# Interleaving the first two tiles of a retention and gMLP layer on eight cores

## The chip, the cores and the metric

The kernel runs on all 8 cores of one Trainium2 chip (trn2). Cores 0 to 3 are on one die, cores 4 to 7 on the other. Each core computes 4 of the 32 sequences and shares nothing with the others. The metric is the device time, in microseconds, of the slowest core.

Engines are named as in the profile: PE is the matmul engine, PEld its weight loads, DVE is VectorE, ACT is ScalarE, POOL is GpSimd, SP issues the DMA transfers. The trace also records the clock that PE was granted, as a share of full speed. A whole run can be in a slow state, with one die's clock clearly lower (in e1's run of 3871.15 us the cores of die 1 had a mean clock of 0.811 to 0.816, those of die 0 0.993 to 0.995); the runs are labelled with it. I call a core **undisturbed** when its mean granted clock over the execution is 0.991 or more, and an execution undisturbed when all eight cores are.

## The reference, cut to what matters

```python
D_MODEL, BATCH, SEQ, DEPTH = 1024, 32, 2048, 1
def reference(x, p, g_mix, w_in, ret_norm_g, sg_norm_g, w_s, b_s, w_out, ...):
    h = rmsnorm(x, g_mix[i])
    q, k, v, g, u, sv = jnp.split(h @ w_in[i], cuts, axis=-1)      # six columns of 512
    q = rotary(q.reshape(B, S, 4, 128), pos)
    k = rotary(k.reshape(B, S, 4, 128), pos) * 128 ** -0.5
    r = chunk_retention(q, k, v)                                   # recurrent over chunks
    r = layernorm_nogain(r).reshape(B, S, 512) * ret_norm_g[i]
    y_ret = jax.nn.silu(g) * r
    y_sg = spatial_gating(gelu(u), gelu(sv), w_s[i], b_s[i], sg_norm_g[i])
    x = x + jnp.concatenate([y_ret, y_sg], axis=-1) @ w_out[i]
    x = x + jnp.square(relu(rmsnorm(x, g_ffn[i]) @ w_ff1[i])) @ w_ff2[i]
    ...                                                            # gated embedding, final rmsnorm
```

## The kernel before

A core's 8192 tokens are 16 tiles of 512. Each tile goes through a *mixer* (the six projections of 512 columns, retention, gating), an output projection, a feed-forward and a gate. Weights come as *units* of 1024x512. On its first use a unit is read in float32 (2 MB, four *stage* pieces of 512 KB), multiplied by the norm's gain, converted to bf16 into a *ring* buffer, and written back to memory as bf16 (1 MB); later uses read those.

The program is scheduled on the host: every operation has a wanted time `vt`, the engines that may do it with a guessed duration, and the buffers it needs. A list scheduler simulates the engines and emits one fixed instruction order for each. Two things follow. Wanted times are priorities and not times on the chip. And any change of a duration or of an allowed engine reorders instructions everywhere.

The core of the scheduler. A DMA is a candidate as soon as its inputs and its buffer allow; nothing limits how far the queue runs ahead of the transfers:

```python
DMA_BW = 265e3
...
                    if op.ready > now + 1e-9:
                        continue
                    if e in op.lock and port[0] > now + 1e-9:
                        continue
                    if not can_alloc(op, now):
                        continue
```

The load of a unit: four pieces, the scaling on DVE or ACT (`both`), the write-back 20 us after in priority:

```python
        def load_unit(name, vt, cache=None):
            ...                                             # cut: ring buffer, cache of the first tiles
                for i in range(4):
                    s = g.buf("stage")
                    dma(lambda s=s: ap(s), lambda i=i: wf_d[u, :, i * 1024:(i + 1) * 1024], [], [(s, 0)], vt, ...)
                    if name in GAIN:
                        for j in range(2):
                            ...
                            g.add(both(512,
                                       lambda e, ...: e.tensor_scalar(
                                           out=o_(), in0=i_(), scalar1=gT[:, gc:gc + 1], scalar2=None, op0=ALU.mult),
                                       lambda e, ...: e.activation(
                                           out=o_(), in_=i_(), func=AF.Copy, scale=gT[:, gc:gc + 1])),
                                  [(s, 0), c("gT")], [(b, (i, j))], vt + 1, lock=("dve",))
                ...
                dma(lambda: wb_d[u], lambda: ap(b).rearrange("p k n -> p (k n)"), UB(b), [(wb_buf[name], 0)],
                    vt + 20, lambda: ("ws" + ring, b.slot), 1048576)
```

The projections of q and k, with the rotary: three products of a PSUM result on DVE and one sum on GpSimd for each of the eight heads:

```python
            for name, base in (("q", 0), ("k", 4)):
                u = load_unit(name, vt[0] - 25, cache)
                for h in range(4):
                    p = g.buf("psum")
                    g.add(mmgroup(lambda p=p: ps(p), lambda k, u=u, h=h: ap(u)[:, k, h * 128:(h + 1) * 128],
                                  lambda k: ap(n1T)[:, k, :], 8), UB(u) + A1, [(p, 0)], vt[0])
                    ...
                    g.add({"dve": (0.69, ... ap(m1) = ps(p) * cos            )}, ...)      # shortened
                    g.add({"dve": (0.69, ... ap(m2)[0:64] = ps(p)[64:] * sin )}, ...)
                    g.add({"dve": (0.69, ... ap(m2)[64:] = ps(p)[:64] * -sin )}, ...)
                    g.add({"pool": (1.27, ... ap(o) = ap(m1) + ap(m2)        )}, ...)
```

The normalisation of the retention result, on DVE, and the gain and gate products on GpSimd:

```python
                g.add({"dve": (1.6, nrm)}, [(bo, 0), (s2, "mv"), (s2, "r")], [(rn, 0)], vt[0])
                YR[b] = g.buf("y")
                g.add({"pool": (1.27, lambda e, o=YR[b]: e.tensor_tensor(out=ap(o), in0=ap(rn), in1=ap(GS[b]),
                                                                       op=ALU.mult))}, ...)
```

The order of the program: tile 0's mixer, tile 1's mixer, one output projection and one feed-forward for both, then a steady loop.

```python
        mixer(0, -195.0, 65.0, cache, True)
        mixer(1, -130.0, 65.0, cache, True)
        outproj([0, 1], -60.0, 50.0, True)
        ffn([0, 1], 0.0, 270.0)
        mixer(2, 30.0, 160.0)
        ...
```

## Time and profile before

| what | value | from |
|---|---|---|
| time, three runs | 3254.9, 3258.37, 3886.76 us | the runs; the last is slow |
| span of the undisturbed cores of the profiled execution (0 to 3) | 3236.9 us | cores, median |
| PE busy from 300 to 3100 us, core 1 | 2754.0 of 2800 us | busy time by stretch |
| first matmul, core 1 | 39.15 us | timeline of PE |
| start of the feed-forward, median of cores 0 to 3 | 196.2 us | trace: weight load number 805 |
| PE idle before that, median | 60.4 us | trace |

"Start of the feed-forward" is used through the whole document. All kernels here do the same 804 weight loads in the first two mixers and their output projection, so the start of the 805th marks the same point of the work in each.

The span and mean granted clock of each core, of the profiled execution before:

```profile
core 1: 3238.6 us, clock 0.994
...
die 0 (median of its cores): 3236.9 us, clock 0.994
die 1 (median of its cores): 3278.0 us, clock 0.980
```

Die 1 was disturbed, so core 1 is what I read. Its busy time by stretch; the columns are the stretch and its length, then busy us (and instructions) of PE, PEld, DVE, ACT and POOL, the granted PE clock, the busy share of the DMA engines, and GB/s:

```profile
0.00:40.00 40.00, 0.85 (x3) 0.32 (x4) 2.54 (x8) 18.19 (x26) 2.33 (x7) 1.00 0.91 268
40.00:160.00 120.00, 97.17 (x566) 49.30 (x565) 92.93 (x252) 59.67 (x89) 51.90 (x45) 0.93 0.86 262
160.00:199.00 39.00, 38.59 (x239) 19.82 (x238) 28.36 (x68) 24.69 (x38) 12.05 (x13) 1.00 0.47 163
300.00:3100.00 2800.00, 2754.01 (x14674) 1322.96 (x14673) 1638.19 (x3300) 988.10 (x1545) 593.37 (x550) 1.00 0.55 188
```

The last line is the steady state: PE is busy 98% of it, so it is bound by matmuls. The first three are the start: PE is idle for nearly all of the first 40 us, and for 22.8 of the next 120.

Why the first matmul is late is in the timeline of the DMA issues (start us, length of the issue, queue, line, operation, out<-in, count):

```profile
5.54 2.72 SPq L502 DMA_DIRECT2D xb<-x  x4
...
11.03 6.48 SPq L502 DMA_DIRECT2D xb<-x  x4
...
18.47 20.88 SPq L502 DMA_DIRECT2D stage<-wf  x8
39.40 0.54 SPq L502 DMA_DIRECT2D wb<-ring  x1
```

The first weights (wf) go out behind eight x blocks of 512 KB each, and the first write-back (wb) follows at once, while DMA is the scarce resource (busy share 0.91 in the first 40 us, 0.86 in the next 120). After the first matmul, PE waits for these, from 40 to 199 us on core 1 (who waits <- who is waited for: us in total, times, longest; the four largest):

```profile
PE ps L629 <- POOL qk L724: 7.4, 2, 7.0
PE ps L804 <- ACT Sbf L832: 5.7, 3, 2.2
PE ps L629 <- DVE y L945: 2.9, 2, 1.5
PE ps L804 <- DVE st L840: 2.7, 1, 2.7
```

L724 is the rotary sum on GpSimd, L832 a copy of the retention state, L945 the gating product, L840 a part of the normalisation.

### The profile page before, as it was taken

The numbers are of one execution on the slowest core, as the hardware profiler recorded it, in microseconds if no ns is written. First come the engines' busy times: TensorE is split into PE (matmuls) and PEld (weight loads), VectorE is DVE, ScalarE is ACT, GpSimd is POOL, SyncE is SP. The second block draws the span as 40 slices with busy tenths as digits, with TensorE's granted clock in tenths as the row PEclk, the third lists the DMA queues.
The fourth block names the chain that finished last, engine by engine and source line by source line (L and its number), as shares of the span: only waits on it lengthen the run. The fifth ranks groups of instructions, "written<-read, shape, count | busy, mean of one in ns | idle before, by whom it ended". The sixth has DMA issues, their size and how long they took to land.

```text
span 3281.8 us, 48876 instructions; the slowest of 8 cores (3231.4 to 3281.8 us)
## 1 busy us (share of the span) xinstructions
PE 3168.4 (97%) x16592; PEld 1511.0 (46%) x16592; DVE 1876.3 (57%) x3799; ACT 1185.6 (36%) x1837; POOL 681.9 (21%) x635
## 2 busy tenths in 40 slices
PE   4899998999999999999999999999999999999998
PEld 2444443444444444444444444444444444444444
DVE  3856656646556474564736656375564745647444
ACT  4563535233233332333324233342333323332233
POOL 1512102302213121131302213022130211313001
PEclk9899998999999999999999999999999999999999
DMA  9757755545546464464645546455464644645442
GB/s 275 240 194 249 255 191 195 210 152 199 186 172 214 147 220 167 166 224 155 219 154 180 199 161 221 160 183 202 169 208 149 217 164 177 218 154 187 149 170 86
DMA packets 113858, 618.31 MB, mean 188 GB/s; under 512 B 13136, under 2 KB 13392, under 8 KB 63440
## 3 DMA queue, kind: packets, MB, share of 16 engines
q1 hardware_dynamic: 113616, 615.19, 54.6%
q8 instruction: 139, 2.28, 0.3%
q14 instruction: 103, 0.84, 0.1%
HBM read 554.32 MB, written 60.82 MB: 187 GB/s over the span
## 4 chain that ended last, share of the span: by engine, by line
PE 94%; DMA 2%; ACT 1%; DVE 1%; issue 1%; SPq 1%; POOL 0%; DVEq 0%; ACTq 0%; POOLq 0%
PE ps L621 89%; PE ps L629 3%; DMA stage<-wf 2%; SPq L502 1%; ACT rel L1048 0%; PE ps L936 0%; PE ps L768 0%; PE ps L804 0%; PE ps L816 0%; PE ps L806 0%; ACT scr L927 0%; DVE TG L884 0%; ACT ring L577 0%; ACT ring L588 0%; DMA xb<-x 0%
## 5 line engine op out<-in xcount | busy, mean ns | idle before, releaser
L621 PE MATMUL ps<-TG,ring 128*128 128x512 bf16 x5120 | 1188.4, 386 | 56.2 <-ACT ring L577 39.3
L621 PE MATMUL ps<-ring,TG 128*128 128x512 bf16 x4096 | 984.0, 385 | 20.7 <-ACT rel L1048 10.7
L621 PE MATMUL ps<-ring,hT 128*128 128x512 bf16 x4096 | 926.7, 380 | 0.0
L621 PEld LDWEIGHTS ps<-TG,ring 128*128 128x128 bf16 x5120 | 501.0, 99 | 655.4 <-issue 140.1
L621 PEld LDWEIGHTS ps<-ring,TG 128*128 128x128 bf16 x4096 | 399.5, 99 | 498.6 <-issue 90.0
L1052 DVE TENSOR_TENSOR hT<-rel 128x512 bf16<-128x512 f32 x457 | 374.6, 820 | 420.8 <-ACT rel L1048 418.1
L621 PEld LDWEIGHTS ps<-ring,hT 128*128 128x128 bf16 x4096 | 395.4, 98 | 449.6 <-issue 11.7
L1048 ACT ACTIVATE rel<-ps 128x512 f32<-128x512 f32 x512 | 304.8, 596 | 755.3 <-PE ps L621 749.6
L1075 DVE SCALAR_TENSOR_TENSOR xb<-ps,st,xb 128x512 f32<-128x512 f32 x288 | 215.3, 747 | 275.6 <-PE ps L621 274.6
L724 POOL TENSOR_TENSOR qk<-scr 128x512 bf16<-128x512 f32 x128 | 163.8, 1280 | 873.7 <-DVE scr L721 873.7
L636 ACT ACTIVATE xsb<-xb 128x1024 bf16<-128x1024 f32 x200 | 210.5, 1052 | 330.2 <-DVE xb L1075 231.3
L1052 POOL TENSOR_TENSOR hT<-rel 128x512 bf16<-128x512 f32 x55 | 57.2, 1040 | 621.2 <-ACT rel L1048 621.1
L1119 ACT ACTIVATE gt<-ps,st 128x512 f32<-128x512 f32 x128 | 87.7, 686 | 220.2 <-PE ps L621 212.7
L993 DVE TENSOR_TENSOR xb<-xb,ps 128x512 f32<-128x512 f32 x128 | 87.8, 687 | 126.9 <-PE ps L621 120.0
L1125 DVE SCALAR_TENSOR_TENSOR gt<-gt,ps 128x512 f32<-128x512 f32 x128 | 87.8, 687 | 79.9 <-ACT gt L1119 78.7
L715 DVE TENSOR_TENSOR scr<-ps,rot 128x512 f32<-128x512 f32 x128 | 88.3, 690 | 67.9 <-PE ps L621 66.8
L871 POOL TENSOR_TENSOR y<-scr 128x512 bf16<-128x512 f32 x64 | 89.6, 1400 | 137.3 <-DVE scr L866 136.9
L1024 ACT ACTIVATE TG<-ps 128x1024 bf16<-128x1024 bf16 x75 | 76.7, 1024 | 108.9 <-PE ps L629 91.9
L945 DVE SCALAR_TENSOR_TENSOR y<-ps,bsT_s,scr 128x128 bf16<-128x128 f32 x256 | 72.0, 344 | 52.7 <-ACT scr L927 26.9
L788 POOL TENSOR_TENSOR scr<-scr,retgh 128x512 f32<-128x512 f32 x64 | 81.6, 1275 | 92.0 <-DVE scr L785 91.9
L905 ACT ACTIVATE scr<-ps,st 128x512 f32<-128x512 f32 x64 | 43.6, 687 | 157.5 <-PE ps L621 157.5
L866 DVE TENSOR_SCALAR scr<-ps,st 128x128 f32<-128x128 f32 x256 | 87.3, 405 | 18.7 <-POOL st L857 18.7
(79 smaller groups left out, 2379.0 us busy)
## 6 DMA issues: line engine op xcount, KB each, us to landing
ring<-wb SPq DMA_DIRECT2D x366, 1024.0 KB, 5.5
stage<-wf SPq DMA_DIRECT2D x104, 512.0 KB, 8.1
stage<-xT SPq DMA_DIRECT2D x64, 512.0 KB, 7.4
xb<-x SPq DMA_DIRECT2D x64, 512.0 KB, 5.5
out<-xb SPq DMA_DIRECT2D x64, 512.0 KB, 3.7
stage<-x SPq DMA_DIRECT2D x56, 512.0 KB, 10.8
wb<-ring SPq DMA_DIRECT2D x26, 1024.0 KB, 9.3
rot<-ROT SPq DMA_DIRECT2D x16, 512.0 KB, 6.1
```

The costliest lines, as they stand in the source:

```text
L621: r = e.matmul(out(), lhs(k), rhs(k), start=(start + k == 0), stop=(start + k == total - 1))
L629: r = e.transpose(out=psb(outb)[:, k * 128:(k + 1) * 128], in_=srcf(k), identity=ident[:, :])
L636: g.add({"act": (t_act(1024) + 0.19, lambda e: e.activation(out=ap(j), in_=ap(xbuf), func=AF.Square, accum_out=acc()))}, [(xbuf, 0), (xbuf ...
L715: g.add({"dve": (0.69, lambda e, p=p, m1=m1: e.tensor_tensor(out=ap(m1), in0=ps(p), in1=ap(rotb)[:, 0, :], op=ALU.mult))}, [(p, 0), (rotb, ...
L724: g.add({"pool": (1.27, lambda e, m1=m1, m2=m2, o=o: e.tensor_tensor(out=ap(o), in0=ap(m1), in1=ap(m2), op=ALU.add))}, [(m1, 0), (m2, 0), ...
L871: g.add({"pool": (1.27, lambda e, o=YR[b]: e.tensor_tensor(out=ap(o), in0=ap(rn), in1=ap(GS[b]), op=ALU.mult))}, [(rn, 0), (GS[b], 0)], [( ...
L993: g.add({"dve": (0.69, lambda e, p=p, xx=xx, hsl=hsl: e.tensor_tensor(out=ap(xx)[:, hsl], in0=ap(xx)[:, hsl], in1=ps(p), op=ALU.add))}, [( ...
L1048: g.add({"act": (t_act(512), lambda e, p=p, r=r: e.activation(out=ap(r), in_=ps(p), func=AF.Relu))}, [(p, 0)], [(r, 0)], vt[0])
L1052: fsq = lambda e, r=r, o=o: e.tensor_tensor(out=ap(o), in0=ap(r), in1=ap(r), op=ALU.mult)
L1075: e.scalar_tensor_tensor(out=ap(xx)[:, hsl], in0=ps(fbb), scalar=stc(s4, 8 + b), in1=ap(xx)[:, hsl], op0=ALU.mult, op1=ALU.add))},
L1119: g.add({"act": (t_act(512) + .1, lambda e, p=p, gt=gt, b=b: e.activation(out=ap(gt), in_=ps(p), func=AF.Tanh, scale=stc(st, 12 + b)))}, [ ...
L1125: g.add({"dve": (0.69, lambda e, p2=p2, gt=gt: e.scalar_tensor_tensor(out=ap(gt), in0=ap(gt), scalar=1.0, in1=ps(p2), op0=ALU.add, op1=ALU ...
```

## The change

The intent is to shorten the start. q's weights and tile 0's transposed x go out first, q's matmuls run by quarters as the pieces land, and the two mixers are interleaved so that each unit that arrives feeds two tiles. Write-backs are put off until the weights are in. The scheduler holds a DMA back while more than 4 us of transfers are queued, so that priorities decide what goes out. Tile 1's rotary and the retention's normalisation may leave DVE, and GpSimd may scale weights too. Line numbers of the kernel after are shifted against those of before: its matmuls are L627 (before L621), its transposes L635 (before L629). Not shown in the cut: a third rotary table, other buffers for tile 1's q, k and v, and a small DVE operation per block that prepares the bias for the normalisation on ACT.

```diff
+DMA_AHEAD = 4.0
@@ the scheduler
+                    if op.dma is not None and dma_free[0] > now + DMA_AHEAD:
+                        heapq.heappush(events, dma_free[0] - DMA_AHEAD)
+                        continue
@@ constants and identity: wanted 15 to 20 us later
-        cload("KD", KD[:, :], KD_d[:, :], VT0 - 10)
+        cload("KD", KD[:, :], KD_d[:, :], VT0 + 10)
@@ load_unit
-                    dma(... wf_d[u, :, i * 1024:(i + 1) * 1024], [], [(s, 0)], vt,
+                    dma(... wf_d[u, :, i * 1024:(i + 1) * 1024], [], [(s, 0)],
+                        vt + (2 * i if name == "q" else 0),
...
-                            g.add(both(512, <dve>, <act>),
-                                  [(s, 0), c("gT")], [(b, (i, j))], vt + 1, lock=("dve",))
+                            g.add(both(512, fts, <act>, fts),                       # fts: DVE or GpSimd
+                                  [(s, 0), c("gT")], [(b, (i, j))], vt + 1, lock=("dve", "pool"))
...
-                    vt + 20, lambda: ("ws" + ring, b.slot), 1048576)
+                    vt + (80 if cache is not None else 20), lambda: ("ws" + ring, b.slot), 1048576)
@@ mixer
+                pieces = t == 0 and name == "q"
+                if pieces:
+                    for i in range(4):
+                        for h in range(4):
+                            g.add(mmgroup(..., 2, start=2 * i, total=8),
+                                  [(u, (i, 0)), (u, (i, 1)), (n1T, i)], [(P4[h], 0)], vt[0] + i)
...
+                    if early and t:                                                 # tile 1's rotary
+                        for i in range(2):
+                            g.add({"act": (t_act(512), ... ap(m2)[lo, :] = ps(p)[hi, :])}, ...)
+                        g.add({"pool": (1.27, ... ap(m2) = ap(m2) * rot(1))}, ..., lock=("pool",))
+                    else:
                         <the two DVE products as before>
...
+                def nrma(e):
+                    for h in range(4):
+                        r = e.activation(out=ap(rn)[:, hs], in_=ps(bo)[:, hs], func=AF.Identity,
+                                         scale=stc(s2, 36 + h), bias=stc(s2, h))
-                g.add({"dve": (1.6, nrm)}, [(bo, 0), (s2, "mv"), (s2, "r")], [(rn, 0)], vt[0])
+                g.add({"dve": (1.6, nrm), "act": (1.2, nrma)}, [(bo, 0), (s2, "mv"), (s2, "r"), (s2, "s6")], [(rn, 0)],
+                      vt[0])
@@ the program
-        mixer(0, -195.0, 65.0, cache, True)
-        mixer(1, -130.0, 65.0, cache, True)
+        mixer(0, -195.0, 100.0, cache, True, xs_vt=-3.0, xt_vt=-30.0)
+        mixer(1, -185.0, 125.0, cache, True, "hT", "hT", xs_vt=-2.0, xt_vt=-28.0)
```

## The prediction

> **What bounds the kernel now.** On core 1, an undisturbed die, the span is 3238.6 us. Busy time by stretch shows TensorE (PE) busy 2754 of the 2800 us from 300 to 3100 us: matmul-bound, DMA at 55%. The start is not. From 0 to 199 us, where the first feed-forward matmul starts, PE is busy 136.6 us and idle 62.4:
> - 39.2 us before the first matmul. The waits put it on the scaling of the first weight unit; the timeline of DMA issues shows why: rotary table, eight x blocks and constants (about 6.5 MB) go out ahead of the q weights, which follow from 18.5 us, with DMA already at 97-100%.
> - about 23 us in pieces up to 160 us: 7.0 on the GpSimd add of the rotary, 5.7 on the state copy, 2.7 on normalisation, the rest on transposes and sums. VectorE is 96% busy in many 5 us slices; DMA is 91-97% busy from 20 to 100 us, at 266-298 GB/s.
>
> **What the change does.**
> 1. q weights and transposed x go first, each quarter of q used as it lands. Only about 2 MB must land before the first matmul. Estimate from 290 GB/s, 1.5 us of issue, 0.7 us of scaling: first matmul at 11-13 us, tile 0's q done at 22-25. That q runs at DMA rate, then tile 1's transposed x (2 MB, 7 us) is awaited: 20-26 us of PE idle by 40 us, against 39.
> 2. Interleaving gives each 2 MB unit (7.3 us of DMA) eight groups (13.9 us of PE), so PE, not DMA, should pace from about 35 us.
> 3. Deferred write-back moves 6 MB (about 21 us of DMA) behind the last unit; DMA is now nearly idle at 160-170 and 190-213 us. Moved, not saved; the feed-forward after it runs at 234-312 GB/s.
> 4. Tile 1's rotary: 16 VectorE products of 0.69 us become 16 ScalarE copies[...] and 8 GpSimd products of 1.28 us. The normalisation (1.6 us of VectorE per block) may go to ScalarE. VectorE, 124 us busy in the first 199, should fall to 100-113; GpSimd, 66, should rise to 76 or more. A q or k unit costs GpSimd 4x1.27 + 4x2.55 = 15.3 us, more than PE's 13.9: some waiting moves there.
>
> Steady state gains little; the 9 us stop near 500 us (x buffers awaiting output) is untouched.
>
> [...] granted clock 0.50 at 60-65 us, after a 7 us gap.
>
> **On the critical path.** Ideally, PE-paced after 35 us, the feed-forward starts near 158 us (41 saved). Dependencies through VectorE and GpSimd, and DMA shared with write-backs, should give back about 10. I expect it near 167 us: 32 us saved.
>
> **Predicted time: 3226 us, range 3206 to 3246.** All startup idle is 62 us, 1.9%, so over 2% is nearly out of reach. Faster by over 2%: 0.03; within 2%: 0.96; slower: 0.01.
>
> **What would show it.** Step 1: first matmul at 10-14 us. Step 2: PE idle in 40-160 us at 8-15 us instead of 23. Step 3: no write-backs before about 80 us. Step 4: VectorE below 113 us busy in the first 199 us, GpSimd above 75. Sum: the same later stages, about 32 us earlier.
>
> **What would make it wrong.** GpSimd or ScalarE becomes the pacer; the capped DMA lookahead starves the queue; deferred write-backs hold ring buffers, so later weights are late and the gain is given back by 400 us; or the changed instruction order moves steady-state stalls.

Two passages are cut, where marked: an estimate for ScalarE's copies (measured in after: 0.59 us each, L749, core 1) and a sentence on the clock; the granted clock of 0.50 beside it is from the trace of before. The forecast's sum: 199 - 158 = 41 us ideally, about 10 given back, 32 us saved, and 3258.37 - 32 = 3226 us. Figures close to those of the estimate in point 1 are in the trace of before, core 1: 289 GB/s from 40 to 60 us, the first transposed x issued at 1.51 us, 0.71 us for a scaling on ACT (L577). So are those of point 2: 2.1 MB at 289 GB/s are 7.3 us, and 64 matmuls at the pace of the 40 from 117.42 us (0.216 us each) are 13.8 us.

## The result, and the profile after

Four runs of the changed kernel took 3222.24 to 3224.33 us, median 3223.7, all fast and all undisturbed. The kernel before took 3254.9 and 3258.37 us in its two fast runs; its other two, 3620.93 and 3886.76, were slow. The ratio of after to before is 0.9898 (0.9874 to 0.9922). Ratios here are the mean time of one kernel's fast runs over that of the other's fast runs of the same rounds, so they are not quite the ratios of the medians that I quote.

**That ratio is not like for like.** On the chip of experiment e6, the fast runs of the kernel before took 3255.7 to 3264.0 us, and in each of them at least one pair of cores ran at clock 0.985 to 0.987 while the others had 0.993 to 0.996. In the run of 3260.45 us, cores 0 and 1 had spans of 3258.9 and 3258.1 us at 0.985 and cores 2 to 7 spans of 3233.5 to 3239.8 us. Where no pair was disturbed, the same kernel took 3240.7 to 3245.6 us (16 executions on several chips), median 3243.4. The four runs of the kernel after carry no disturbed core. The clocks of the first two runs of before were not kept, so that they had such a pair is inferred from their length. Undisturbed against undisturbed, the gain is 3243.4 - 3223.7 = 19.7 us, 0.6%, and not 33. A repeat on a chip where before ran undisturbed gave that directly: ratio 0.994 (after_again, below).

The two dies of the profiled execution after, and core 1 by the same stretches as before:

```profile
die 0 (median of its cores): 3219.7 us, clock 0.994
die 1 (median of its cores): 3221.1 us, clock 0.993
```

```profile
0.00:40.00 40.00, 17.64 (x63) 6.84 (x63) 13.43 (x19) 17.59 (x21) 7.90 (x11) 0.91 0.91 262
40.00:160.00 120.00, 102.87 (x625) 52.35 (x624) 86.73 (x257) 79.61 (x134) 89.12 (x74) 0.94 0.84 257
160.00:199.00 39.00, 39.00 (x230) 19.65 (x229) 21.40 (x38) 29.78 (x47) 7.47 (x5) 1.00 0.80 253
300.00:3100.00 2800.00, 2752.42 (x14633) 1320.68 (x14631) 1576.03 (x3138) 1043.13 (x1730) 573.60 (x539) 1.00 0.54 188
```

The steady state has not moved (2752.4 us of PE against 2754.0). The first 40 us gained 16.8 us of PE. From 40 to 160 us PE gained only 5.7, while GpSimd went from 51.9 to 89.1 us busy and ACT from 59.7 to 79.6.

The DMA issues of core 1 after:

```profile
1.50 1.36 SPq L507 DMA_DIRECT2D stage<-xT  x3
2.91 1.58 SPq L507 DMA_DIRECT2D stage<-wf  x1
4.54 0.67 SPq L507 DMA_DIRECT2D rot<-ROT  x1
10.79 0.33 SPq L507 DMA_DIRECT2D stage<-xT  x1
11.72 5.14 SPq L507 DMA_DIRECT2D stage<-wf  x3
...
51.70 0.33 SPq L507 DMA_DIRECT2D stage<-IDENT  x1
...
63.76 0.58 SPq L507 DMA_DIRECT2D wb<-ring  x1
```

The order is the one intended, and the first write-back is now issued at 63.8 us. But nothing is issued between 41.1 and 51.7 us: the queue waits 7.3 us for ACT and 3.2 us for GpSimd to convert pieces and so free stage buffers, and the transfers fall to 164 GB/s from 50 to 60 us. What PE did in that time on core 1 (start us, length, then the idle time before it and its releaser):

```profile
16.64 3.57 PE L627 MATMUL ps<-TG,ring 128*128 128x512 bf16 x8 [16.64 <-ACT ring L583]
20.66 5.84 PE L627 MATMUL ps<-TG,ring 128*128 128x512 bf16 x24 [0.44 <-ACT ring L583]
31.77 22.64 PE L627 MATMUL ps<-TG,ring 128*128 128x512 bf16 x96 [5.27 <-ACT TG L681]
```

q of tile 0 is done at 26.5 us; then PE waits 5.3 us for tile 1's transposed x, the input of the next matmuls. After that, its waits are spread over many lines (40 to 179 us, core 1; the four largest):

```profile
PE ps L635 <- POOL y L925: 4.9, 3, 2.5
PE ps L627 <- ACT scr L919: 2.9, 1, 2.9
PE ps L856 <- DVE Sst L867: 1.6, 1, 1.6
PE ps L627 <- DVE ring L580: 1.3, 1, 1.3
```

The wait of 7 us is gone. At the head are now GpSimd's product of gate and normalised retention (L925) and the normalisation that the change put on ACT (L919).

The account over all undisturbed cores, medians, in us (4 cores before, 8 after); medians of parts do not add up exactly to the median of the whole. "Lost to the clock" is the time before the feed-forward times the part of the clock that was not granted. It is an upper bound of the cost, since PE is idle for part of these stretches; the line under it counts only the time in which PE was busy.

| | before | after | difference |
|---|---|---|---|
| first matmul | 38.9 | 15.1 | -23.8 |
| PE idle, 0 to 40 us | 38.9 | 21.7 | -17.2 |
| PE idle, 40 to 130 us | 16.5 | 16.5 | 0.0 |
| PE idle, 130 us to the feed-forward | 4.6 | 0.2 | -4.4 |
| PE busy until the feed-forward | 136.6 | 140.4 | +3.8 |
| (lost to the clock) | 8.5 | 10.2 | +1.7 |
| (lost to the clock while PE was busy) | 5.3 | 8.4 | +3.1 |
| **start of the feed-forward** | **196.2** | **178.6** | **-17.6** |
| from there to the end | 3039.7 | 3042.0 | +2.3 |
| DVE / ACT / POOL busy until the feed-forward | 123.6 / 102.5 / 66.2 | 111.2 / 110.2 / 102.5 | |

So some 17 of the 22 us of idle time saved come from the first 40 us, none from the 90 us in which the interleaving was to work, 4.4 us from the last stretch, and 3.8 us are given back in busy time, most of it (3.1 us) at a lowered clock.

### The profile page after: what moved, and what is told of

It is laid out like the page before. It is cut to its first block, busy times and chain, and to the rows that moved or that the text cites. A ratio compares the mean times of both kernels' runs of the same rounds, so it can differ in the third digit from the quotient of the medians.

```text
span 3222.5 us, 49142 instructions; the slowest of 8 cores (3216.9 to 3222.5 us)
## 1 busy us (share of the span) xinstructions
PE 3125.9 (97%) x16592; PEld 1498.3 (46%) x16592; DVE 1813.2 (56%) x3636; ACT 1244.8 (39%) x2045; POOL 716.0 (22%) x662
## 4 chain that ended last, share of the span: by engine, by line
PE 93%; DMA 2%; ACT 1%; POOL 1%; issue 1%; DVE 1%; SPq 0%; DVEq 0%; ACTq 0%; POOLq 0%
PE ps L627 89%; PE ps L635 3%; DMA stage<-wf 1%; DMA stage<-xT 1%; ACT rel L1102 0%; DMA xb<-x 0%; PE ps L990 0%; PE ps L808 0%; PE ps L844 0%; POOL ring L580 0%; PE ps L846 0%; PE ps L856 0%; ACT scr L981 0%; ACT scr L919 0%; POOL y L925 0%
## 5 line engine op out<-in xcount | busy, mean ns | idle before, releaser
L627 PE MATMUL ps<-TG,ring 128*128 128x512 bf16 x5120 | 1164.5, 380 | 38.9 <-ACT ring L583 16.8
L627 PE MATMUL ps<-ring,TG 128*128 128x512 bf16 x4096 | 974.2, 382 | 24.4 <-ACT rel L1102 10.7
L627 PE MATMUL ps<-ring,hT 128*128 128x512 bf16 x4096 | 923.2, 379 | 0.0
L627 PEld LDWEIGHTS ps<-TG,ring 128*128 128x128 bf16 x5120 | 495.6, 98 | 622.6 <-issue 48.8
L627 PEld LDWEIGHTS ps<-ring,TG 128*128 128x128 bf16 x4096 | 396.9, 98 | 494.4 <-issue 44.9
L627 PEld LDWEIGHTS ps<-ring,hT 128*128 128x128 bf16 x4096 | 393.7, 98 | 442.9
L764 POOL TENSOR_TENSOR qk<-scr 128x512 bf16<-128x512 f32 x120 | 154.5, 1287 | 855.3 <-DVE scr L761 792.1
L1047 DVE TENSOR_TENSOR xb<-xb,ps 128x512 f32<-128x512 f32 x128 | 87.9, 687 | 127.5 <-PE ps L627 120.8
L755 DVE TENSOR_TENSOR scr<-ps,rot 64x512 f32<-64x512 f32 x120 | 83.2, 693 | 63.6 <-PE ps L627 62.6
L925 POOL TENSOR_TENSOR y<-scr 128x512 bf16<-128x512 f32 x64 | 81.5, 1274 | 161.3 <-ACT scr L919 156.1
L919 ACT ACTIVATE scr<-ps,st 128x128 f32<-128x128 f32 x224 | 84.3, 459 | 69.0 <-DVE st L902 69.0
L828 POOL TENSOR_TENSOR scr<-scr,retgh 128x512 f32<-128x512 f32 x64 | 81.2, 1269 | 92.3 <-DVE scr L825 89.7
L975 POOL TENSOR_TENSOR svn<-scr,sgg_s 128x512 bf16<-128x512 f32 x64 | 81.7, 1276 | 69.5 <-DVE scr L971 59.8
```

What stands on the lines that cost most here:

```text
L627: r = e.matmul(out(), lhs(k), rhs(k), start=(start + k == 0), stop=(start + k == total - 1))
L755: g.add({"dve": (0.69, lambda e, p=p, m2=m2: e.tensor_tensor(out=ap(m2)[0:64, :], in0=ps(p)[64:128, :], in1=rot(1)[64:128, :], op=ALU.mult))},
L764: g.add({"pool": (1.27, lambda e, m1=m1, m2=m2, o=o: e.tensor_tensor(out=ap(o), in0=ap(m1), in1=ap(m2), op=ALU.add))}, [(m1, 0), (m2, 0), ...
L919: r = e.activation(out=ap(rn)[:, hs], in_=ps(bo)[:, hs], func=AF.Identity, scale=stc(s2, 36 + h), bias=stc(s2, h))
L1047: g.add({"dve": (0.69, lambda e, p=p, xx=xx, hsl=hsl: e.tensor_tensor(out=ap(xx)[:, hsl], in0=ap(xx)[:, hsl], in1=ps(p), op=ALU.add))}, [( ...
```

## The experiments

The theory: the early start is set by the order of the DMA queue, and the interleaving does free PE of its data waits, but the work it brings together overloads GpSimd, which carries the rotary of tile 1, the gain and gate products and now also weight scaling; so the waits moved. Rivals: ACT, which got the copies and the normalisation; the length of the dependent chain of small operations in each block; and the fixed instruction order itself. Each experiment has one edit, or two that were tried alone before. Of all kernels the table gives the medians of the undisturbed cores of the one profiled execution. The median time is of undisturbed executions, where there were any. All kernels gave correct results, except h1, h2 and h3, whose results are wrong on purpose.

| kernel | first matmul | feed-forward starts | PE idle 0-40 | PE idle 40-130 | lost to clock | POOL busy | time |
|---|---|---|---|---|---|---|---|
| before | 38.9 | 196.2 | 38.9 | 16.5 | 8.5 | 66.2 | 3243.4 |
| after | 15.1 | 178.6 | 21.7 | 16.5 | 10.2 | 102.5 | 3223.7 |
| after_again | 16.5 | 178.4 | 22.6 | 17.1 | 9.3 | 102.2 | 3224.9 |
| e3_no_cap | 15.8 | 195.9 | 36.4 | 16.0 | 11.1 | 97.6 | 3241.1 |
| e9_before_cap | 22.7 | 195.0 | 23.8 | 21.2 | 13.7 | 66.7 | 3239.7 |
| e4_sequential | 16.1 | 186.8 | 22.5 | 16.1 | 11.9 | 102.0 | 3233.0 |
| e5_wb_early | 15.8 | 181.2 | 21.0 | 17.4 | 9.3 | 105.2 | 3228.7 |
| e2_rot_dve | 16.1 | 180.0 | 21.6 | 16.8 | 10.2 | 97.3 | 3225.1 |
| e7_no_pieces | 22.6 | 176.8 | 23.1 | 17.1 | 5.1 | 102.3 | 3222.9 |
| e1_no_pool_scale | 16.3 | 177.1 | 22.3 | 14.1 | 11.1 | 77.0 | 3222.5 |
| e6_nrm_dve | 15.9 | 174.5 | 22.5 | 13.8 | 5.9 | 103.4 | 3217.4 |
| e6_again | 15.9 | 173.7 | 22.1 | 13.9 | 5.1 | 103.5 | 3219.4 |
| f1_no_pool_nrm_dve | 15.2 | 176.1 | 21.6 | 13.6 | 9.3 | 76.3 | 3220.0 |
| f3_nrm_dve_pace85 | 16.0 | 178.4 | 22.4 | 13.8 | 11.1 | 109.8 | 3220.3 |
| h1_chain_cut | 15.9 | 172.1 | 22.4 | 13.8 | 5.1 | 103.2 | 3217.3 |
| h2_pool_light | 15.9 | 167.8 | 22.4 | 9.7 | 4.2 | 87.9 | 3210.4 |
| h3_act_light | 15.8 | 173.1 | 21.6 | 13.4 | 5.1 | 103.5 | 3218.1 |
| g1_nrm_dve_no_pieces | 22.4 | 173.6 | 23.4 | 14.9 | 3.4 | 103.7 | 3217.5 |
| g2_fold | 15.7 | 177.3 | 21.3 | 14.9 | 7.7 | 98.2 | 3222.9 |
| g3_fold_no_pool_scale | 15.9 | 170.2 | 21.9 | 10.6 | 6.8 | 66.2 | 3212.9 |

The start of the feed-forward repeats within about 1 us (178.6 and 178.4; 174.5 and 173.7), so differences under 1 us are not read.

### after_again: the change, unaltered

> The changed kernel, unaltered, to measure the gain between executions of like state. The two traces, die 0 against die 0, differ by 17 us of span (3236.9 to 3219.7), while the timed fast runs differ by 33 us (3254.9 and 3258.4 against 3223.7). Theory 'baseline': the fast runs of before that were timed first carried some 15 us of a slower state, and an undisturbed execution of before takes about 3240 us, so the ratio in like state is about 0.9945. Rival: the whole 33 us are real (ratio 0.990) and the trace of before misleads.

Ratio 0.994 (0.9925 to 0.9956), on a chip on which the kernel before ran undisturbed in five of its executions (3242.7 to 3245.6 us). The gain of 1.0% of the first comparison does not repeat; 0.6% does.

### e3_no_cap and e9_before_cap: the limit on the DMA lookahead

```diff
e3_no_cap, against after:
-DMA_AHEAD = 4.0
+DMA_AHEAD = 1e6
e9_before_cap, against before:
+DMA_AHEAD = 4.0
+                    if op.dma is not None and dma_free[0] > now + DMA_AHEAD:
+                        heapq.heappush(events, dma_free[0] - DMA_AHEAD)
+                        continue
```

> The changed kernel without the cap on how far ahead transfers are issued. If the cap is what keeps x blocks and constants behind the q weights, the first matmul goes from 15 us back to 25 us or later, and the feed-forward starts later than 178 us by 5 us or more. Rival: the order given by the changed times of need is enough, the cap only starves the queue (DMA 66-73% busy at 50-60 us), and without it the feed-forward starts earlier.

> The kernel before with nothing but the cap on how far ahead transfers are issued. If the cap alone brings the q weights forward, the first matmul comes at 20-25 us instead of 38.8 and the feed-forward some 8-12 us earlier than 196 us; then most of what step 1 gained needs neither interleaving nor pieces. Rival: without interleaving the earlier q only exposes later waits for weights, and the feed-forward starts within 3 us of 196.

Without the limit nothing of the change is left: ratio to before 0.9991 (0.9973 to 1.0009), the feed-forward at 195.9 us. The timeline of PE on core 1 of e3:

```profile
16.61 3.57 PE L627 MATMUL ps<-TG,ring 128*128 128x512 bf16 x8 [16.61 <-ACT ring L583]
42.70 6.74 PE L627 MATMUL ps<-TG,ring 128*128 128x512 bf16 x24 [22.52 <-ACT ring L583]
```

The first eight matmuls come as early as in the change, but the other three quarters of q were issued at 24.6 us, behind all eight x blocks and the constants, and PE waits 22.5 us for them. (The expectation of a late first matmul was wrong; that of a late feed-forward held.) Without a limit, the scheduler fills the queue with whatever is possible at once, and a more wanted DMA that must first wait for a stage buffer, as q's later pieces do, lines up behind it; with the limit, room is kept for it. The limit is what makes the priority count. The limit alone, on the kernel before, brings the first matmul to 22.7 us, and yet the feed-forward starts at 195.0, 1.2 us earlier: of the 15.1 us of idle time saved by 40 us, 4.7 come back from 40 to 130, some 2 behind that, and some 7 as busy time, of which 5.3 are lost to the clock while PE was busy (10.6 against 5.3). So its rival expectation held: the earlier q only exposed later waits. Ratio 0.9986 (0.9965 to 1.0008). So the limit is necessary and not sufficient.

### e4_sequential, e5_wb_early, e2_rot_dve: three other parts, each undone

```diff
e4_sequential:
-        mixer(0, -195.0, 100.0, cache, ...)
-        mixer(1, -185.0, 125.0, cache, ...)
+        mixer(0, -195.0, 65.0, cache, ...)
+        mixer(1, -130.0, 65.0, cache, ...)
e5_wb_early:
-                    vt + (80 if cache is not None else 20), lambda: ("ws" + ring, b.slot), 1048576)
+                    vt + 20, lambda: ("ws" + ring, b.slot), 1048576)
e2_rot_dve (and the table loaded with it):
-                    if early and t:
+                    if False:
```

> The changed kernel, but the two mixers one after the other again (times of need of the kernel before); cap, early q, pieces, deferred write-back and second rotary stay. If interleaving carries the gain, each 2 MB unit feeds 7 us of PE instead of 14 and PE waits for weights in 20-100 us: PE idle up to the feed-forward rises from 38 to 50 or more and the feed-forward starts at 188 us or later instead of 178.5. Rival: the early, capped transfers carry it, and the feed-forward starts within 3 us of 178.5.

> The changed kernel with the write-back of the weights at its old time. If 1 MB write-backs among the first loads cost their DMA time (about 3.5 us each, 3 to 4 of them before 80 us), the feed-forward starts 5 us or more later than 178.5. Rival: DMA has room (SyncE issues nothing from 41 to 52 us) and it starts within 2 us.

> The changed kernel with tile 1's rotary back on VectorE (three products, as tile 0). If the move relieved the engine that paces, VectorE, by 11 us, the feed-forward starts 4 us or more later than 178.5. If GpSimd and ScalarE are as tight as VectorE, so that the move only changed places, it starts within 2 us. If GpSimd, in program order, is the pacer after all, it starts earlier by 3 us or more.

The interleaving is worth 186.8 - 178.6 = 8.2 us. It isn't earned where it was looked for: without it the idle time from 40 to 130 us is 16.1 us, the same, and the difference is mainly 5.7 us of idle behind 130 us and 1.8 us of busy time. So the start moved about as a useful interleaving demanded, but the idle time did not. The deferred write-back is worth 2.6 us, between what the two theories expected. The second rotary is worth 1.4 us: undoing it puts 13 us back on DVE (124.4 us busy) and takes 14 us off ACT and 5 us off GpSimd, and little happens. Ratios are 0.9928, 0.9921 and 0.9963, against runs of before that all had a disturbed pair (and e2 itself had one undisturbed execution only), so they are not compared with each other.

### e7_no_pieces: the first unit used as a whole

```diff
-                pieces = t == 0 and name == "q"
+                pieces = False
```

> The changed kernel, but tile 0's q groups wait for the whole unit, as before. If using q by quarters is worth something, the feed-forward starts later than 178.5 us by up to the 5 us of PE work that the pieces do before the last quarter is there. Rival: tile 0's q ends at 26 us and tile 1's transposed x comes only at 31.8 us, so PE waits there anyway; without pieces q ends at about 31 us, and the feed-forward moves by less than 1.5 us, although the first matmul moves from 15 to about 23 us.

The first matmul moves from 15.1 to 22.6 us, and the feed-forward starts 1.8 us *earlier* (176.8). On core 1 q's work of both tiles then runs in one stretch, 128 matmuls from 23.05 to 53.4 us. The early quarters of q had bought nothing, as the wait for tile 1's transposed x, which ends at 31.8 us in after, takes back what they gain; in e7 no such wait is left. And they cost: in after the clock is halved at 28.5 us, in that wait and behind it, and in e7 it stays at 1.00 there. Granted clock in three stretches of the kernel after, core 1 (it is the figure before the last two):

```profile
28.50:35.30 6.80, 3.53 (x9) 1.35 (x10) 6.41 (x9) 2.78 (x3) 4.20 (x4) 0.50 0.98 263
103.60:110.40 6.80, 5.65 (x22) 2.66 (x23) 1.66 (x9) 3.84 (x9) 4.79 (x4) 0.50 0.93 268
124.10:130.90 6.80, 4.96 (x15) 2.03 (x16) 3.81 (x15) 3.24 (x7) 4.73 (x4) 0.50 0.85 203
```

At a clock of 0.50, such a stretch of 6.8 us costs 3.4 us of full speed if PE is busy in all of it; by PE's busy time these three cost some 1.8, 2.8 and 2.5 us. Only the first has to do with q's quarters: core 1 of e7 still has the other two, from 103.3 and 123.8 us, and a short one at 76.0. e7 loses 5.1 us before the feed-forward, the change 10.2 (4.0 and 8.4 while PE was busy); why the later stretches are shorter on other cores of e7 was not shown. In after every halved stretch before the feed-forward lasts 3.41 or 6.83 us, on all eight cores; in before, on cores 0 to 3, 3.41, 6.83 or 10.24 us. On core 1 of after the clock was halved at 103.6 and 124.1 us in waits of 2.46 and 2.90 us; in the 3.4 us before, PE had been busy for 1.1 and 1.0 us. What decides when the clock is halved was not tested.

### e1_no_pool_scale and e6_nrm_dve: two permissions withdrawn

```diff
e1_no_pool_scale:
-                                           ... scale=gT[:, gc:gc + 1]), fts),
-                                  ..., lock=("dve", "pool"))
+                                           ... scale=gT[:, gc:gc + 1])),
+                                  ..., lock=("dve",))
e6_nrm_dve, e6_again:
-                g.add({"dve": (1.6, nrm), "act": (1.2, nrma)}, [(bo, 0), ...
+                g.add({"dve": (1.6, nrm)}, [(bo, 0), ...
```

> The changed kernel, but GpSimd may not take part in scaling the weights; that goes back to VectorE and ScalarE. Theory GpSimd: from 50 to 110 us GpSimd, 92-100% busy in 10 us slices, paces the two mixers, and its weight scalings at 1.57 us each (17 or so) are the part it can lose; PE idle in 40-130 us on die 0 should fall from 16.8 to 11 or less and the feed-forward should start at 170-174 us instead of 178. Rival DMA: supply and order of transfers pace it; PE idle and the start of the feed-forward move by less than 2 us. A third outcome: ScalarE or VectorE, given the work back, paces instead, and the feed-forward starts later than 178 us.

> The changed kernel with the normalisation of the retention output on VectorE only. In the steady state ScalarE now takes it (224 of 256 slices); GpSimd's product then waits for ScalarE and PE idles 0.65 and 0.97 us for it in places, and the part after the feed-forward's start is 2.1 us longer than before (3041.8 against 3039.7 on die 0). If that comes from this choice, this part falls back to about 3039.7; if not, it stays near 3041.8. At the start, the feed-forward moves by less than 3 us either way.

> The changed kernel with the normalisation on VectorE only, run again: its undisturbed die started the feed-forward at 174.5 us, against 178.5 of the changed kernel, and its undisturbed executions took 3217.1 to 3219.5 us against 3222.2 to 3225.6. If that is real, the same numbers come again, at every core with a granted clock above 0.992; if it was the chip, they fall together with those of the changed kernel.

Both are better than the change as a whole, at the start of the feed-forward by 1.5 and by 4.1 us (4.9 in the repeat), and in time: 3220.7 to 3223.5 and 3217.1 to 3220.1 us, against 3222.2 to 3225.6. So two of its parts work against it. The weight scaling on GpSimd is dear. All uses of the scaling line before the feed-forward, core 1 of after (count; ns min/median/max, first and last start):

```profile
L580 POOL TENSOR_SCALAR ring<-stage,gT_s x17: 1559/1567/2069, 49.8 to 173.5; 128x512 bf16<-128x512 f32 x17
L580 DVE TENSOR_SCALAR ring<-stage,gT_s x12: 473/487/1434, 15.7 to 176.2; 128x512 bf16<-128x512 f32 x12
```

GpSimd takes 1.57 us for what DVE does in 0.49, and longer than for a product of two 128x512 inputs (1.27 us, L828). Seventeen of these put 27.6 us on GpSimd, the largest single item of its load there; the prediction had not counted them. But taking them away (POOL busy 102.5 to 77.0) gained only 1.5 us, where the theory had asked for 4 to 8, a first mark against it. Why the normalisation is better on DVE, though DVE gets busier by 9 us, is partly seen: PE's wait for L919 goes, and the clock lost halves from 10.2 to 5.9 and 5.1. More was not shown. e6 had been made for another question, whether this normalisation lengthens the part behind the feed-forward's start; that part was 3040.4 and 3041.7 us (after: 3042.0), so it does not.

The profiled execution of e6_nrm_dve carries another find. Cores 0 and 1 had spans of 3243.0 and 3244.3 us, cores 4 to 7 of 3213.0 to 3216.0. The stretch in which they differ, core 0 first, then core 4:

```profile
23.70:290.00 266.30, 257.54 (x1205) 117.27 (x1204) 170.08 (x392) 133.02 (x204) 119.62 (x96) 0.81 0.79 243
```

```profile
23.70:290.00 266.30, 244.80 (x1345) 119.98 (x1369) 186.28 (x431) 145.64 (x223) 128.26 (x104) 0.98 0.84 263
```

Cores 0 and 1 were held at a granted clock of 0.81 for 257 and 255 us on end, apart from the short halved stretches that all cores have; cores 2 and 3 of the same die had a stretch of 0.81 of 112 and 114 us near the end; cores 4 to 7 had none. That is what a disturbed pair is, and why only undisturbed cores enter my tables.

### f1_no_pool_nrm_dve, f3_nrm_dve_pace85, g1_nrm_dve_no_pieces: combinations

```diff
f1: e1 and e6 together.      g1: e6 and e7 together.
f3, against e6:
-        mixer(0, -195.0, 100.0, cache, ...)
+        mixer(0, -195.0, 85.0, cache, ...)
```

> Both: no weight scaling on GpSimd and the normalisation on VectorE only. If the two small gains add (1 to 2 us and 4 us), the feed-forward starts at 172.5 to 173.5 us. If VectorE, given back both, becomes the pacer (it would be busy some 125 us of 175), it starts later than 176 us.

> The normalisation on VectorE only, and tile 0 ordered to run ahead of tile 1 a little more (its times of need stretch over 85 us instead of 100). If the waits of PE between 40 and 130 us, which no single engine's relief removed (16.8 us in the changed kernel, 14 without GpSimd's scaling, 13.7 with the normalisation on VectorE), hang on the order of instructions in the queues, the order alone moves them by 3 us or more either way. If they hang on the load of the engines, which is the same here, they stay within 1.5 us of 13.7 and the feed-forward within 1.5 us of 174.5.

> The changed kernel with the normalisation on VectorE only and q used as a whole. Leaving out pieces moved the feed-forward from 178.3 to 176.8 us (less time at half clock: 5-6 us lost instead of 8.5-12), the normalisation from 178.3 to 174. If both add, it starts at 172-173 us and undisturbed executions take 3216-3218 us, the best of all; if the clock loss is already gone with the normalisation (5-6 us there too), it stays at 174.

The gains do not add. f1 has 27 us less on GpSimd than e6 and is 2 us *slower* (176.1 against 174). g1 is no better than e6. f3 changes nothing but wanted times in the source, and its idle time from 40 to 130 us (13.8) is that of e6; yet its feed-forward starts 4.3 us later, with 11.1 us lost to the clock instead of 5.1 to 5.9. It is no test of order alone, though: the scheduler also put 22 weight scalings on GpSimd before the feed-forward instead of 17, so GpSimd carries 109.8 us instead of 103.4. So a recomputed schedule, order and load together, moved the start by some 4 us; what order alone does was not measured. Any edit that moves a load also reorders, because the order is computed anew, and effects of this size can't be told from it. That left the theory and its rivals open.

### h1_chain_cut, h2_pool_light, h3_act_light: same order, one load or wait less

These keep the instruction order of e6 exactly, since the scheduler is given e6's durations and dependences; the traces agree, every engine and the DMA queue run the same sequence as in e6. What the chip then has to do is made less, at the price of wrong results.

```diff
h1, against e6: the two normalisations of the first two tiles read constants (KD) in place of the block's
    statistics, and don't wait for them:
-    scalar1=mv()[:, h, 0:1], scalar2=stc(s2, 36 + h)
+    scalar1=KD[:, h:h + 1], scalar2=KD[:, h:h + 1]         # dependence exchanged after scheduling
h2, against e6: 64 of 512 columns for two GpSimd products of the first two tiles:
-    out=ap(m2), in0=ap(m2), in1=rot(1), op=ALU.mult
+    out=ap(m2)[:, 0:64], in0=ap(m2)[:, 0:64], in1=rot(1)[:, 0:64], op=ALU.mult
-    out=ap(gs), in0=ap(gs), in1=retgh[:, :], op=ALU.mult
+    out=ap(gs)[:, 0:64 if early else 512], ...
h3, against e6: 128 of 1024 columns for ACT's sums of squares of x in the first two tiles.
```

> Wrong result on purpose. The version with the normalisation on VectorE only; in the first two tiles the two normalisations read constants instead of the mean and root just computed, so every instruction, its order and its size stay, but normalising no longer waits for statistics, VectorE's small sums and GpSimd's power. If this chain holds PE, PE idle in 40-130 us falls from 13.8 to 8 or less and the feed-forward starts at 169 us or earlier instead of 174. If the engines' load holds it, both stay within 1.5 us.

> Wrong result on purpose. The version with the normalisation on VectorE only; in the first two tiles 16 GpSimd products of 1.27 us work on 64 of 512 columns, order unchanged, about 16 us less of GpSimd's 103. If GpSimd in program order paces PE, idle in 40-130 us falls from 13.8 to 9 or less and the feed-forward starts 4 us or more before 174. If it only has more slack now, less than 1.5 us.

> Wrong result on purpose. The version with the normalisation on VectorE only; the eight sums of squares of the first two tiles on ScalarE work on 128 of 1024 columns, order unchanged, about 7 us less of ScalarE's 102. If ScalarE in program order, with weights and statistics in one queue, delays the release of the stage buffers and so the transfers, the feed-forward starts 3 us or more before 174. Otherwise less than 1.5 us.

| against e6 and e6_again (feed-forward 174.5, 173.7; idle 40-130 13.8, 13.9) | feed-forward | idle 40-130 |
|---|---|---|
| h1, normalisation chain cut | 172.1 | 13.8 |
| h2, GpSimd 16 us lighter | 167.8 | 9.7 |
| h3, ACT 6 us lighter | 173.1 | 13.4 |

With the order held fixed, GpSimd's load does set the pace: 15.6 us less of it brings the feed-forward 6.3 us forward (from the mean 174.1), 4.2 us of it as idle time from 40 to 130 us. The chain is worth about 2 us, ACT about 1 us, no more than the scatter of the repeats (but for 6 us of load only). Stretches from 40 to 130 us, core 4 of e6, then core 4 of h2:

```profile
40.00:130.00 90.00, 75.74 (x469) 38.78 (x477) 74.55 (x217) 57.38 (x94) 71.63 (x60) 0.98 0.87 275
```

```profile
40.00:130.00 90.00, 80.91 (x515) 41.52 (x512) 76.92 (x234) 62.85 (x102) 62.29 (x63) 1.00 0.94 287
```

So the theory stands in that GpSimd's load sets the pace, and its size is about 6 us for 16 us of load. By which way is not separated: in h2 the same first 318 DVE instructions also took 136.6 us in sum, against 140.7 and 141.2 in e6 and its repeat, so part of the gain can be that DVE runs faster beside a lighter GpSimd, and not that PE waits less for GpSimd's own results. In after, core 1, a 128x4 operation on DVE (L891) took 224 to 1308 ns before the feed-forward, 700 in the median, and 214 ns in the median from 300 to 3100 us; but with as much on GpSimd the median was 221 ns in e6_nrm_dve (core 4; up to 669). No experiment set such an effect apart from other causes. That f1 and e1 had shown so little can lie in the recomputed order, or in the load that went back to DVE (busy 122.2 us in f1, 120.0 in e6_again); which it was there was not followed up.

### g2_fold and g3_fold_no_pool_scale: the same load off GpSimd, with right results

The retention gain need not multiply the gate on GpSimd (L828, 8 times 1.27 us before the feed-forward). It is per column, so it can scale the rows of the output weights when these are converted, work that DVE or ACT does anyway.

```diff
g2, against e6:
-    retg_d = din("retg_b", [128, 512])
+    retg_d = din("retgT", [128, 4])
-                g.add({"pool": (1.27, ... ap(gs) = ap(gs) * retgh)}, ...)
-                    if name in GAIN:
+                    if name in GAIN or (name in ("o0", "o1") and i < 2):
...
+                            gsrc, gname = (gT, "gT") if name in GAIN else (retgh, "retgh")
g3: g2 and e1 together.
```

> Correct result. The version with the normalisation on VectorE only, and the retention gain applied to the rows of the output weights while they are converted, so that GpSimd's product of the gate by the gain goes (8 x 1.27 us in the first two tiles, 64 in all). If GpSimd's load paces the start, the feed-forward starts at 169-171 us instead of 174 and undisturbed executions take 3212-3215 us. If the new order of instructions undoes it, as with the scaling, it stays at 173-177 us.

> Correct result. The same, and no weight scaling on GpSimd: GpSimd about 66 us busy before the feed-forward instead of 103. If GpSimd is the only pacer, the feed-forward starts at 168 us or earlier. If VectorE and ScalarE, which get the scaling back, pace as soon as GpSimd does not, it starts no earlier than g2.

g2 alone is 3 us later than e6 (177.3), with only 5 us less on GpSimd, as the scheduler filled it with scaling, and 7.7 us lost to the clock. g3 puts GpSimd back to 66.2 us, its load in the kernel before: feed-forward at 170.2 (between its two expectations), idle from 40 to 130 us 10.6, and 3212.5 to 3213.1 us undisturbed. It is correct, and beats both kernels: 10.8 us under after, and 30.5 us, 0.9%, under before (ratio 0.9896, 0.9852 to 0.994, on a chip where before ran mostly undisturbed; one disturbed run of 3277.7 us is in that ratio).

Where it comes from shows in three slices of 10 us on core 1 (columns as in the stretches above; GpSimd is the fifth busy figure). First before, then after, then g3:

```profile
70.00:80.00 10.00, 8.67 (x56) 4.38 (x54) 5.19 (x20) 5.28 (x9) 1.01 (x1) 1.00 0.83 247
80.00:90.00 10.00, 5.47 (x45) 3.15 (x43) 10.00 (x41) 6.27 (x10) 6.22 (x5) 0.92 0.87 222
90.00:100.00 10.00, 9.66 (x39) 4.25 (x40) 8.01 (x27) 4.97 (x8) 6.39 (x6) 0.74 1.00 311
```

```profile
70.00:80.00 10.00, 8.15 (x53) 4.19 (x52) 7.71 (x25) 7.82 (x14) 9.88 (x8) 1.00 0.99 287
80.00:90.00 10.00, 8.70 (x70) 5.02 (x69) 8.96 (x35) 7.17 (x14) 9.20 (x7) 1.00 0.88 281
90.00:100.00 10.00, 7.60 (x55) 4.11 (x54) 7.72 (x26) 6.12 (x13) 9.41 (x9) 1.00 1.02 276
```

```profile
70.00:80.00 10.00, 9.90 (x61) 5.16 (x62) 8.60 (x31) 8.83 (x16) 4.27 (x5) 1.00 0.99 288
80.00:90.00 10.00, 7.34 (x54) 3.90 (x52) 9.74 (x38) 5.78 (x10) 4.36 (x4) 0.89 0.98 270
90.00:100.00 10.00, 8.77 (x67) 4.96 (x66) 9.88 (x35) 4.76 (x8) 2.62 (x3) 0.94 1.08 267
```

Before, DVE is the full engine in the middle slice (10.00 of 10). After, it is GpSimd, with 28.5 of 30 us, and PE reaches 24.4 of 30. In g3, GpSimd has room, DVE is nearly full again, and PE reaches 26.0.

## Why the prediction was right or wrong

**The time was right by luck: two errors cancel.** 3226 was predicted, 3223.7 measured. The predicted saving of 32 us was counted from 3258.37, a time that, judged by its length, carries a disturbed pair of cores (inferred, as said above). From the undisturbed 3243.4, 32 us would have given 3211. The baseline was some 15 us too high, the saving 12 us too large (19.7 measured over the run, 17.6 at the feed-forward). What the prediction got wrong is therefore the saving: "I expect it near 167 us" was 178.6. Its own parts, with idle of 20 to 26 us by 40 us and of 8 to 15 us from 40 to 160, add up to 21 to 34 us less than the 62.4 us of core 1; the 32 came from an ideal of 158 us and sat at the upper end of that.

**Step 1, first matmul and the first 40 us: nearly right.** Predicted 10 to 14 us; measured 15.1. On core 1, three pieces of x, the first of the weights and the rotary table share the DMA engines from the start (2.5 MB), and q's first quarter landed only at 15.5 us. Tile 0's q done at 22 to 25 was 26.5. The wait for tile 1's transposed x (5.3 us) and the idle time by 40 us (21.7, predicted 20 to 26) were right. What was not seen: using q piece by piece earns nothing behind that wait, and e7 shows that the kernel is 1.8 us quicker at the feed-forward without it. It was also taken for a matter of order alone; e3 shows that, though the first matmul stays early without it, the gain by 40 us (21.7 us idle, 36.4 in e3) hangs on the limit of the lookahead, which the prediction names only as a risk.

**Step 2, "PE, not DMA, should pace from about 35 us": failed.** This is the step that broke. PE's idle time from 40 to 160 us on core 1 went from 22.8 to 17.1 us, not to 8 to 15: 5.7 us saved where 8 to 15 were forecast; from 40 to 130 us it did not move (16.5 and 16.5, medians). The interleaving removed waits of 7.0 and 5.7 us and made new ones, on GpSimd above all. The prediction had costed GpSimd at 15.3 us for a q or k unit against 13.9 of PE, and noted that "some waiting moves there", but left out seventeen weight scalings of 1.57 us. GpSimd's load before the feed-forward rose from 66.2 to 102.5 us, where "76 or more" was forecast, and some 27 us of that are the scalings. h2 shows 6 us of pace for 16 us of GpSimd load at equal order. "GpSimd or ScalarE becomes the pacer" was in the list of what would make it wrong; for GpSimd it did, and for ScalarE h3 shows about 1 us. Nor had the prediction any term for the clock, though it had noted a granted clock of 0.50 at 60-65 us: what the clock cost while PE was busy grew from 5.3 to 8.4 us, and busy time by 3.8 us.

**Step 3, write-backs not before about 80 us: failed, little lost.** The first was issued at 63.8 us (39.4 before). The deferral is worth 2.6 us (e5). The risk named with it was not the one seen: the queue did starve, from 41.1 to 51.7 us, for stage buffers that ACT and GpSimd were slow to free. How much that stop costs was not tested.

**Step 4, DVE below 113 us busy in the first 199, GpSimd above 75: half right.** On core 1 DVE was 121.6 us busy in the first 199 us, though only about 111 before the feed-forward, which now starts sooner; GpSimd was 104.5, against "76 or more". That shift was taken for a relief. e2 and e6 show that the rotary's part is worth 1.4 us and the normalisation's minus 4 us.

**Steady state: right.** 2752.4 against 2754.0 us of PE in 2800. The part behind the feed-forward's start is 2.3 us longer in after than before; across the variants it is 3038.7 to 3042.2 us. Among kernels with the order of after or e6 it goes with the clock: every core has a stretch of halved clock near 480 us, and in e6_again the cores where this lasted 13.65 us needed 3041.6 to 3042.0 us, those where it lasted 6.83 us 3039.0 and 3039.4. All eight cores of after had 13.65 us. But cores 0 and 1 of before had 13.65 us too and needed only 3039.1 and 3039.7, so the difference to before stays open, as do the many small waits that are left from 40 to 130 us in the best kernel (10.6 us), and what decides when a pair of cores loses its clock.

## What to carry to other kernels

Before a gain of under 1% is predicted, read the cores of the baseline one by one: two cores at a lower clock (0.985) added some 16 us, most of the change's whole gain of 19.7, to a run that counted as fast (3260.45 us against 3243.4). When a change spreads work over more engines, add up each engine's load in the stretch concerned with its own durations, every alternative that the scheduler may choose included: a weight scaling that took 0.49 us on DVE here took GpSimd 1.57. And where instruction order is computed from loads, test a suspected load at a fixed order, with less work in the same instructions, before a load is acquitted, and then ask what else that lighter load sped up.
